# Moving ten weight splits from attention into the input stage of a hybrid attention and convolution trunk

## The chip, the cores and the metric

The kernel runs on one core of one Trainium2 chip. The metric is the device time of one execution in microseconds (us), as the median over several runs. The engines are named as in the profile: PE is TensorE's matrix unit (PEld its weight loads), DVE is VectorE, ACT is ScalarE, POOL is GpSimd, and SP is SyncE, which here issues nearly all transfers.

## The reference, cut to what matters

There are two layers over 1024 tokens of width 1024, each with a pre-norm and a residual add, and a final RMSNorm. The first layer is gated latent attention with 8 heads, the second a gated convolution module.

```python
z = h @ w_in                                   # layer 0: latents, rotary key, gate
q = (rmsnorm(q_lat, q_norm_g) @ w_qb)          # 8 heads of 128 + 64 rotary
kv = (rmsnorm(kv_lat, kv_norm_g) @ w_kvb)
o = causal_block_attention(q, k, v)
x = x + (o * silu(gate)) @ w_out
a, b, gate = split(h @ w_in + b_in, 3)         # layer 1: three projections
u = depthwise_conv31(a * sigmoid(b)) + dw_b
u = silu(layernorm(u, ln_g, ln_b))
x = x + (u * silu(gate)) @ w_out + b_out
return rmsnorm(x, final_norm_g)
```

What bears on the change are two weight matrices of layer 1: the gate columns of its input projection, in eight blocks called `cg0` to `cg7` (`wc[16]` to `wc[23]`), and its output projection, in eight blocks `e0` to `e7` (`we[0]` to `we[7]`). Each block is 128 by 1024 numbers of 4 bytes, 512 KB.

## The kernel before

**Two halves of every operand.** For precision each operand of a product is held as a high half in a rounded format (`hi`) and a low half, the difference (`lo = raw - hi`). A product is then three matmuls, `wh*xh`, `wh*xl` and `wl*xh`, at L138, L139 and L140 of `mm3`.

**Three ways to get a weight.** `load_w` loads a raw block, makes `hi` on ACT (L105) and `lo` on DVE or POOL (L107), and the halves are used at once. `split_early` (L113) is run long before the block is wanted: it loads the raw block, makes both halves in two pieces of 512 columns (L120 on ACT, L121 on the engine held in `early_eng`), and writes the low half alone to a DRAM tile `loS`. `load_split` is used in the last stages: it loads the raw block and the stored low half, and makes only the high half again (L134). So each of the sixteen blocks `cg0` to `cg7` and `e0` to `e7` is split once early, and its subtraction doesn't have to be done in the last stages.

**The buffers that all of them share.** A raw block takes a slot of tag `wraw`, of which there are 2. A high or low half takes a slot of tag `w`, of which there are 5. A slot is free again when its last reader is done: a raw slot after the subtraction, a high half of a split after the subtraction, a low half of a split after its transfer to DRAM, and the halves of a weight in use after the last matmul that reads them.

**The stages.** The input stage first accumulates the key and value latents over eight blocks of x (tile `acc`). Then come eleven calls of `in_tile`, each a gemm of 48 matmuls of 512 columns (tile `ps_b`) with weights from `w1b`: three for the query latents, then eight for the attention gate in `gate_tile(0)` to `gate_tile(7)`. Between gate tiles 5 and 6 stand two `rope_pair` calls (tile `ps_qr`), which need the normed query latents from `lat_norm` (tiles `Frq`, `rowq`, `Fq`, `zgq`, `qnh`, `qnl`). In this text the gate tiles are called g0 to g7. The attention stage follows: `proj(h)` (tile `pj`, weights `wqk[h]`, tile `wl_qk` for their low half), `score`, and `attend`, for eight heads. Then come the output projection of layer 0, the convolution layer, and the last stages that use `load_split`.

**What sets the order.** In the input stage, and after attention, PE's order is the order in which the code is written. Everywhere else a planner places the instructions on each engine before the program runs. It walks the program with a model of time and gives an engine, or SP's queue, what is ready and has a free slot; of two raw loads that want the same slot, the one written first goes first, as far as the trace before shows it. The order on each engine is then fixed, and an instruction that waits holds up all behind it on its engine.

**Where the splits stand.** Before the change `cg0` to `cg5` are split in the input stage, one behind each of g0 to g5, with `early_eng` on DVE. Behind g7 `early_eng` is set to POOL. `cg6` and `cg7` are split in heads 0 and 1, and `e0` to `e7` in heads 0 to 7, one in each, all on POOL.

Of the kernel before, what the change touches and what calls it, by code (L numbers as in the profile page):

```python
# [64 lines left out]
def hybrid_body(ctx, tc, xT, xP, pos, cols, w1a, w1b, wqr, wqk, wv, wo, wc, we, out):  # L65
    nc = tc.nc
    v, s, g, pe, sp = nc.vector, nc.scalar, nc.gpsimd, nc.tensor, nc.sync
# [28 lines left out]
    early_eng = [v]  # L96

    def load_w(src, n, nm, alloc=None, eng=None):
        if alloc is None:
            def alloc(name):  # L100
                return wp.tile([P, 1024], F32R, tag="w", bufs=5, name=name)
        raw = wp.tile([P, 1024], F32, tag="wraw", name=f"wr_{nm}")
        sp.dma_start(raw[:, :n], src)
        hi = alloc(f"wh_{nm}")
        s.activation(hi[:, :n], raw[:, :n], AF.Copy)  # L105
        lo = alloc(f"wl_{nm}")
        (eng or early_eng[0]).tensor_tensor(lo[:, :n], raw[:, :n], hi[:, :n].bitcast(F32), ALU.subtract)  # L107
        return hi, lo
# [4 lines left out]
    def split_early(src, nm):  # L113
        raw = wp.tile([P, 1024], F32, tag="wraw", name=f"sr_{nm}")
        sp.dma_start(raw, src)
        hi = wp.tile([P, 1024], F32R, tag="w", bufs=5, name=f"sh_{nm}")
        lo = wp.tile([P, 1024], F32R, tag="w", bufs=5, name=f"sl_{nm}")
        for a in range(2):
            cs = sl(a, CH)
            s.activation(hi[:, cs], raw[:, cs], AF.Copy)  # L120
            early_eng[0].tensor_tensor(lo[:, cs], raw[:, cs], hi[:, cs].bitcast(F32), ALU.subtract)  # L121
        loS[nm] = tc.dram_tile([P, 1024], F32, name=f"loS{nm}")
        sp.dma_start(loS[nm], lo.bitcast(F32))
# [13 lines left out]
    def mm3(ps, wh, wl, xh, xl, start, stop):  # L137
        pe.matmul(ps, wh, xh, start=start, stop=False)  # L138
        pe.matmul(ps, wh, xl, start=False, stop=False)  # L139
        pe.matmul(ps, wl, xh, start=False, stop=stop)  # L140
# [67 lines left out]
    def sl(k, n=P):  # L208
        return slice(k * n, (k + 1) * n)
# [23 lines left out]
    def tmp(nm):  # L233
        return ar.tile([P, T], F32, tag="tmp", bufs=4, name=nm)
# [4 lines left out]
    def pacc(nm):  # L239
        return pa.tile([P, CH], F32, tag="acc", bufs=6, name=nm)  # L240
# [72 lines left out]
    def lat_norm(zg, folded, n, gname, dh, dl, nm):  # L313
        F, part = folded
        ps = pstat(f"cs{nm}")[:, :32]
        pe.matmul(ps, mod32, part, start=True, stop=True)
        Fc = inv_sqrt(ps, 1.0 / (n * P), 1e-6, nm, extra=Rc)
        Fr = small.tile([P, 32], F32, tag="Fr", bufs=1, name=f"Fr{nm}")
        v.tensor_tensor(Fr, Fc, Rc, ALU.mult)
        spread_dma(Fr, T, F, nm)  # L320
        for i in range(n):
            v.scalar_tensor_tensor(zg[i], zg[i], cc(gname, i), F, ALU.mult, ALU.mult)
            s.activation(dh[i], zg[i], AF.Copy)
            v.tensor_tensor(dl[i], zg[i], dh[i].bitcast(F32), ALU.subtract)
# [11 lines left out]
    def in_tile(n):  # L336
        wh, wl = load_w(w1b[n], 1024, f"b{n}", eng=v)
        ps = []
        for c in range(2):
            ch = sl(c, CH)  # L340
            ps.append(pacc(f"ps_b{n}{c}"))
            for k in range(KD):
                mm3(ps[c], wh[:, sl(k)], wl[:, sl(k)], xgh[k][:, ch], xgl[k][:, ch],
                    k == 0, k == KD - 1)
        return ps
# [26 lines left out]
    def gate_tile(h):  # L372
        ps = in_tile(NQL + h)
        gt = tmp(f"gt{h}")
        for c in range(2):
            v.tensor_tensor(gt[:, sl(c, CH)], ps[c], R[:, sl(c, CH)], ALU.mult)
        s.activation(gt, gt, AF.Silu)
        sp.dma_start(gateS[h], gt)
# [6 lines left out]
    for h in range(3):  # L385
        gate_tile(h)
        split_early(wc[16 + h], f"cg{h}")
        if h == 2:
            lat_norm(zgq, folded, NQL, "gq", qnh, qnl, "q")

# [46 lines left out]
    def rope_pair(pr):  # L437
        ab = []
        for j in range(2):
            wh, wl = load_w(wqr[2 * pr + j], 384, f"qr{pr}{j}")  # L440
            t_ = ar.tile([P, T], F32, tag="zg", bufs=5, name=f"qr{pr}{j}")
            for c in range(2):
                ch = sl(c, CH)
                ps = pacc(f"ps_qr{pr}{j}{c}")
                for k in range(NQL):
                    mm3(ps, wh[:, sl(k)], wl[:, sl(k)], qnh[k][:, ch], qnl[k][:, ch],
                        k == 0, k == NQL - 1)
                s.activation(t_[:, ch], ps, AF.Copy, scale=QSCALE)
            ab.append(t_)
        A, B = ab  # L450
        for j in range(2):
            t1, t2 = tmp(f"rt1{pr}{j}"), tmp(f"rt2{pr}{j}")
            v.tensor_tensor(t1, A if j == 0 else B, cosT, ALU.mult)
            v.tensor_tensor(t2, B if j == 0 else A, sinT, ALU.mult)
            v.tensor_tensor(t1, t1, t2, ALU.subtract if j == 0 else ALU.add)
            hi = ar.tile([P, T], F32R, tag="rhi", bufs=1, name=f"rh{pr}{j}")
            s.activation(hi, t1, AF.Copy)
            v.tensor_tensor(t2, t1, hi.bitcast(F32), ALU.subtract)
            sp.dma_start(ropeS[j][pr], hi.bitcast(F32))
            sp.dma_start(ropeS[2 + j][pr], t2)  # L460

    for h in range(3, 6):
        gate_tile(h)
        split_early(wc[16 + h], f"cg{h}")
    rope_pair(0)
    rope_pair(1)
    gate_tile(6)
    gate_tile(7)

    early_eng[0] = g  # L470
    es_pe.close()
    es_ap.close()
    es_ax.close()
    es_ar.close()


    early = ctx.enter_context(tc.tile_pool(name="early", bufs=NFIRST, side="right",
                                           reuse_waits="tile"))
    es_b = ExitStack()
# [64 lines left out]
    def score(h, i):  # L544
        q_h, q_l, k_h, k_l, rq, _ = heads[h]
        nk = (i + 1) * P
        ps = psS_p.tile([P, T], F32, tag="S", name=f"S{h}_{i}")
        if i == 0:
            chunks, off = [(0, 256)], 0
        elif i == 4:  # L550
            chunks, off = [(0, 384), (384, 640)], 128
        else:
            chunks, off = [(a, min(a + CH, nk)) for a in range(0, nk, CH)], 0
        qs = sl(i)
        for a, b in chunks:
            o_ = ps[:, off + a : off + b]
            ks = slice(a, b)
            pe.matmul(o_, q_h[:, qs], k_h[:, ks], start=True, stop=False)
            pe.matmul(o_, q_h[:, qs], k_l[:, ks], start=False, stop=False)
            pe.matmul(o_, q_l[:, qs], k_h[:, ks], start=False, stop=False)  # L560
            pe.matmul(o_, rq[:, qs], krh[:, ks], start=False, stop=False)
            pe.matmul(o_, rq[:, qs], krl[:, ks], start=False, stop=True)
        st = b1.tile([P, 3], F32, tag="st", bufs=8, name=f"st{h}_{i}")
        last = ps[:, off + i * P : off + nk]
        v.tensor_tensor(last, last, mask, ALU.add)
        v.tensor_reduce(st[:, 0:1], ps[:, off : off + nk], AX.X, ALU.max, negate=True)  # L566
        pr = b1.tile([P, nk], F32, tag=f"P{i}", bufs=2 if i in (2, 3) else 1, name=f"P{h}_{i}")
        s.activation(pr[:, :nk], ps[:, off : off + nk], AF.Exp, bias=st[:, 0:1],  # L568
                     accum_out=st[:, 1:2])
        v.reciprocal(st[:, 2:3], st[:, 1:2])  # L570
        g.tensor_scalar(pr[:, :nk], pr[:, :nk], st[:, 2:3], 1.0, ALU.mult, ALU.mult)  # L571
        probs[h, i] = pr
# [46 lines left out]
    def load_og(grp, h, c):  # L619
        pair = act_tile(grp, f"og{c}{h}")  # L620
        sp.dma_start(pair[1].bitcast(F32), ogS[h][c])
        split_og(pair[1].bitcast(F32), pair)
        return pair
# [4 lines left out]
    for h in range(NH):  # L628
        for i in range(8):
            score(h, i)  # L630
            if i == 1 and pending is not None:
                attend(*pending)
                pending = None
            if i == 3 and h + 1 < NH:
                proj(h + 1)
            if i == 4 and h < 2:
                split_early(wc[22 + h], f"cg{6 + h}")
            if i == 6:
                split_early(we[h], f"e{h}")
            if i == 5:  # L640
                if h < NH - 1:
                    attend(h, 0)
                else:
                    ogt[0] = [load_og("A", h_, 0) for h_ in range(NH - 1)]
                    ogt[0].append(act_tile("A", f"og0{h}"))
                    attend(h, 0, ogt[0][h])
        pending = (h, 1)
# [499 lines left out]
```

## Time and profile before

| what | value |
|---|---|
| median of 3 runs | 906.93 us (906.04 to 909.69) |
| the profiled execution's own time | 906.78 us |
| its span, first to last instruction | 904.8 us |
| PE busy | 891.2 us, 98% of the span |
| DVE, ACT, POOL busy | 653.1, 503.5, 372.1 us |
| moved by DMA | 110.71 MB, mean 122 GB/s |

The span is what the trace covers, and 2 us of the execution's own time lie around it. PE's busy time overlaps itself, since matmuls are pipelined: a matmul of 512 columns is listed with some 0.40 us, but in a dense run the next one starts 0.23 us later. So the starts of matmuls tell more than the busy share. The input stage ends, and attention begins, with the first matmul of tile `pj`.

### The profile page before, as it was taken

Reading aid. Unit: us, or ns where it says so; the run is one execution under the profiler, and the core shown is the slowest. Engines: PE = TensorE matmul, PEld = TensorE weight load, DVE = VectorE, ACT = ScalarE, POOL = GpSimd, SP = SyncE. Lnnn points to the kernel's source line nnn. Section 1 sums busy time; section 2 is a strip of 40 time slices with the busy share of each in tenths; the row PEclk is TensorE's granted clock in tenths of the full one; section 3 lists DMA queues with packets and bytes.
Section 4 is the critical chain, followed back from the end, with each engine's and each line's share of the span. In section 5 each row is a group of like instructions: output and inputs, shape, how many; then the busy total and the mean of one; then the engine's idle time right before and its main releaser. Section 6 shows DMA issues by size and latency. Waiting matters only on the chain.

```text
span 904.8 us, 12389 instructions
## 1 busy us (share of the span) xinstructions
PE 891.2 (98%) x4416; PEld 743.1 (82%) x4416; DVE 653.1 (72%) x1114; ACT 503.5 (56%) x839; POOL 372.1 (41%) x335
## 2 busy tenths in 40 slices
PE   9999999999999999999999999999999999999996
PEld 7888887888988988988878778888888887778996
DVE  7788857556656666676454968999999997687543
ACT  8535355255645554574443457766666763678732
POOL 0000000143532522642334559999999992000034
PEclk9999999999999999999999999999999999999998
DMA  7325635572422430651363421111113323135714
GB/s 269 116 71 177 222 124 190 194 226 87 142 89 82 141 106 29 231 164 37 111 224 126 141 69 48 47 49 45 47 48 105 95 87 109 51 137 199 255 68 137
DMA packets 39837, 110.71 MB, mean 122 GB/s; under 512 B 5280, under 2 KB 8352, under 8 KB 39776
## 3 DMA queue, kind: packets, MB, share of 16 engines
q1 hardware_dynamic: 39408, 109.27, 36.2%
q8 instruction: 35, 0.57, 0.3%
q10 hardware_dynamic: 288, 0.39, 0.1%
q14 instruction: 26, 0.21, 0.1%
q0 software_dynamic: 80, 0.26, 0.1%
HBM read 83.93 MB, written 24.92 MB: 120 GB/s over the span
## 4 chain that ended last, share of the span: by engine, by line
PE 80%; DVE 3%; DMA 1%; ACT 1%; issue 1%; POOL 0%; DVEq 0%; SPq 0%; ACTq 0%; POOLq 0%
PE e L138 3%; PE e L140 3%; PE cb L139 3%; PE e L139 3%; PE cb L140 3%; PE T L584 3%; PE cb L138 3%; PE cg L138 3%; PE cg L139 3%; PE cg L140 3%; PE ca L138 3%; PE ca L140 3%; PE ca L139 3%; PE o L140 3%; PE o L138 3%; PE o L139 3%
## 5 line engine op out<-in xcount | busy, mean ns | idle before, releaser
L836 POOL TENSOR_TENSOR dcv<-dcv,pkb 128x512 f32<-128x512 f32 (+1 forms) x126 | 157.7, 1254 | 8.6 <-ACT pkb L835 1.0
L835 ACT ACTIVATE pkb<-u,taps 128x512 f32<-128x512 f32 (+1 forms) x126 | 83.6, 673 | 55.7 <-POOL dcv L836 50.9
L571 POOL TENSOR_SCALAR P<-P,st 128x128 f32<-128x128 f32 (+3 forms) x64 | 48.1, 753 | 120.7 <-DVE st L570 112.9
L847 DVE SCALAR_TENSOR_TENSOR av<-u,taps,av 128x512 f32<-128x512 f32 (+1 forms) x135 | 91.9, 689 | 1.2 <-ACT av L841 1.1
L107 POOL TENSOR_TENSOR wl_qk<-wr_qk,wh_qk 128x640 fp32r<-128x640 f32 x8 | 12.6, 1573 | 171.7 <-PE ps_b L139 165.1
L849 DVE SCALAR_TENSOR_TENSOR cv<-su,gsum,cv 128x512 f32<-128x512 f32 (+1 forms) x117 | 80.7, 690 | 0.4
L594 DVE TENSOR_TENSOR ptl<-T,pth 128x512 fp32r<-128x512 f32 (+1 forms) x96 | 52.3, 554 | 32.1 <-ACT pth L593 31.8
L593 ACT ACTIVATE pth<-T 128x512 fp32r<-128x512 f32 (+1 forms) x96 | 46.1, 490 | 52.3 <-PE T L584 45.3
L138 PE MATMUL ps_b<-xgh,wh_b 128*128 128x512 f32 x176 | 69.9, 397 | 0.0
L139 PE MATMUL ps_b<-xgl,wh_b 128*128 128x512 f32 x176 | 69.7, 396 | 0.0
L140 PE MATMUL ps_b<-xgh,wl_b 128*128 128x512 f32 x176 | 69.7, 396 | 0.0
L1026 POOL TENSOR_TENSOR x<-x,rbe 128x512 f32<-128x512 f32 (+1 forms) x16 | 16.2, 1043 | 126.8 <-DMA rbe<-rowe 121.6
L107 POOL TENSOR_TENSOR wl_o<-wr_o,wh_o 128x1024 fp32r<-128x1024 f32 x16 | 42.4, 2662 | 57.5 <-PE o L140 24.4
L138 PE MATMUL e<-a_y,wh_e 128*128 128x256 f32 (+1 forms) x192 | 61.8, 322 | 0.0
L140 PE MATMUL e<-a_y,wl_e 128*128 128x256 f32 (+1 forms) x192 | 61.6, 321 | 0.0
L139 PE MATMUL e<-a_y,wh_e 128*128 128x256 f32 (+1 forms) x192 | 61.4, 320 | 0.0
L568 ACT ACTIVATE P<-S,st 128x128 f32<-128x128 f32 (+3 forms) x64 | 47.5, 741 | 23.4 <-DVE st L566 18.7
L138 PE MATMUL cg<-a_h,wh_cg 128*128 128x512 f32 x128 | 51.7, 404 | 0.0
L139 PE MATMUL cb<-a_h,wh_cb 128*128 128x512 f32 x128 | 50.9, 397 | 0.8 <-DVE a_h L766 0.8
L140 PE MATMUL o<-a_og,wl_o 128*128 128x512 f32 x128 | 51.1, 399 | 0.3 <-POOL wl_o L107 0.3
L138 PE MATMUL o<-a_og,wh_o 128*128 128x512 f32 x128 | 51.0, 400 | 0.0
L138 PE MATMUL ca<-a_h,wh_ca 128*128 128x512 f32 x128 | 50.9, 397 | 0.0
(327 smaller groups left out, 2677.3 us busy)
## 6 DMA issues: line engine op xcount, KB each, us to landing
wr_o<-in_wo_dram SPq DMA_DIRECT2D x16, 512.0 KB, 3.9
wr_e<-in_we_dram SPq DMA_DIRECT2D x14, 512.0 KB, 4.6
wl_e<-loSe SPq DMA_DIRECT2D x14, 512.0 KB, 3.7
wr_b<-in_w1b_dram SPq DMA_DIRECT2D x11, 512.0 KB, 3.3
sr_cg<-in_wc_dram SPq DMA_DIRECT2D x8, 512.0 KB, 4.2
loScg<-sl_cg SPq DMA_DIRECT2D x8, 512.0 KB, 2.9
gateS<-gt SPq DMA_DIRECT2D x8, 512.0 KB, 4.3
rq<-ropeS SPq DMA_DIRECT2D x32, 128.0 KB, 2.8
```

The source lines that it names most:

```text
L107: (eng or early_eng[0]).tensor_tensor(lo[:, :n], raw[:, :n], hi[:, :n].bitcast(F32), ALU.subtract)
L138: pe.matmul(ps, wh, xh, start=start, stop=False)
L139: pe.matmul(ps, wh, xl, start=False, stop=False)
L140: pe.matmul(ps, wl, xh, start=False, stop=stop)
L568: s.activation(pr[:, :nk], ps[:, off : off + nk], AF.Exp, bias=st[:, 0:1], accum_out=st[:, 1:2])
L571: g.tensor_scalar(pr[:, :nk], pr[:, :nk], st[:, 2:3], 1.0, ALU.mult, ALU.mult)
L593: s.activation(hi[:, n0:], pt[:, n0:], AF.Copy)
L594: v.tensor_tensor(lo[:, n0:], pt[:, n0:], hi[:, n0:].bitcast(F32), ALU.subtract)
L835: s.activation(pk, lag(src, i), AF.Copy, scale=tap(of, i))
L836: g.tensor_tensor(acc, acc, pk, ALU.add)
L847: v.scalar_tensor_tensor(a_, lag(E, i), tap(dwe, i), a_, ALU.mult, ALU.add)
L849: v.scalar_tensor_tensor(c_, lag(su, i), tap(gsum, i), c_, ALU.mult, ALU.add)
```

## The change

Ten calls of `split_early` move from the head loop into the input stage. `e0` and `e1` are split behind g1 and g2, `e2` to `e4` behind g3 to g5, `cg6` and `cg7` behind g6 and g7, and `e5`, `e6`, `e7` behind that, with no gate tile between them. All sixteen are then worked out with `early_eng` on DVE. `early_eng` is set to POOL a few lines later than before, still ahead of attention. What each split loads, computes and stores is the same.

```diff
     for h in range(3):
         gate_tile(h)
         split_early(wc[16 + h], f"cg{h}")
+        if h > 0:
+            split_early(we[h - 1], f"e{h - 1}")
         if h == 2:
             lat_norm(zgq, folded, NQL, "gq", qnh, qnl, "q")
...
     for h in range(3, 6):
         gate_tile(h)
         split_early(wc[16 + h], f"cg{h}")
+        split_early(we[h - 1], f"e{h - 1}")
     rope_pair(0)
     rope_pair(1)
-    gate_tile(6)
-    gate_tile(7)
-
-    early_eng[0] = g
+    for h in range(6, 8):
+        gate_tile(h)
+        split_early(wc[16 + h], f"cg{h}")
+    for h in range(5, 8):
+        split_early(we[h], f"e{h}")
+
...
+    early_eng[0] = g
...
             if i == 3 and h + 1 < NH:
                 proj(h + 1)
-            if i == 4 and h < 2:
-                split_early(wc[22 + h], f"cg{6 + h}")
-            if i == 6:
-                split_early(we[h], f"e{h}")
```

## Rows read from the trace of the kernel before

**Rows 1.** The page's first part: busy us, share of the span, instructions.

```profile
PE 891.2 (98%) x4416; PEld 743.1 (82%) x4416; DVE 653.1 (72%) x1114; ACT 503.5 (56%) x839; POOL 372.1 (41%) x335
```

**Rows 2.** Windows: stretch, its us, busy us (instructions) by engine, clock, DMA.

```profile
core 0: us, PE busy (x) PEld busy (x) DVE busy (x) ACT busy (x) POOL busy (x), PEclk, DMA share, GB/s
60.00:180.00 120.00, 119.71 (x514) 96.27 (x514) 87.22 (x122) 52.63 (x69) 3.32 (x4) 1.00 0.51 175
180.00:380.00 200.00, 199.43 (x1183) 175.74 (x1181) 125.84 (x279) 110.63 (x244) 80.65 (x104) 1.00 0.38 120
...
160.00:180.00 20.00, 20.00 (x87) 16.11 (x87) 9.72 (x11) 5.46 (x7) 3.32 (x4) 1.00 0.51 185
```

**Rows 3.** Windows of 4 us at the kernel's start, the busiest for DMA.

```profile
12.00:16.00 4.00, 4.00 (x19) 3.22 (x18) 4.00 (x7) 4.00 (x6) 0.00 (x0) 1.00 1.05 405
```

**Rows 4.** Waits of PE, longest in total first: us, times, longest us.

```profile
PE bce L194 <- DVE rte L187: 1.3, 1, 1.3
```

**Rows 5.** Groups by line and shape: busy us, mean ns, idle before.

```profile
L121 POOL TENSOR_TENSOR sl_e<-sr_e,sh_e 128x512 fp32r<-128x512 f32 x16 | 20.4, 1296 | 2.1 <-ACT sh_e L120 1.1 <-PE pj L139 0.9
L121 DVE TENSOR_TENSOR sl_cg<-sr_cg,sh_cg 128x512 fp32r<-128x512 f32 x12 | 7.8, 687 | 2.0 <-PE ps_b L139 2.0
L120 ACT ACTIVATE sh_cg<-sr_cg 128x512 fp32r<-128x512 f32 x16 | 9.2, 624 | 15.7 <-DMA sr_cg<-in_wc_dram 15.7
L107 DVE TENSOR_TENSOR wl_b<-wr_b,wh_b 128x1024 fp32r<-128x1024 f32 x11 | 13.4, 1221 | 5.4 <-PE ps_b L139 3.0 <-ACT zgkv L328 2.4
L105 ACT ACTIVATE wh_b<-wr_b 128x1024 fp32r<-128x1024 f32 x11 | 11.6, 1056 | 10.3 <-PE acc L304 5.8 <-DMA wr_b<-in_w1b_dram 3.0 <-PE ps_b L140 1.5
L105 ACT ACTIVATE wh_qk<-wr_qk 128x640 fp32r<-128x640 f32 x8 | 5.9, 738 | 10.4 <-PE ps_b L140 8.7 <-DMA wr_qk<-in_wqk_dram 0.9 <-POOL sl_e L121 0.8
L107 POOL TENSOR_TENSOR wl_qk<-wr_qk,wh_qk 128x640 fp32r<-128x640 f32 x8 | 12.6, 1573 | 171.7 <-PE ps_b L139 165.1 <-PE pj L139 5.5 <-ACT wh_qk L105 0.6
```

**Rows 6.** DMA issues: count, KB each, median us from issue to landing.

```profile
sr_cg<-in_wc_dram SPq DMA_DIRECT2D x8, 512.0 KB, 4.2
...
wr_qk<-in_wqk_dram SPq DMA_DIRECT2D x8, 320.0 KB, 3.7
```

**Rows 7.** Tile `sr_e`, raw blocks split in attention: shortest, median, longest landing.

```profile
DMA to landing us min/median/max: 3.3/5.4/6.7
```

**Rows 8.** Timeline of PE: first matmuls of g2, of the rope, of g6, of attention.

```profile
92.72 0.40 PE L138 MATMUL ps_b<-xgh,wh_b 128*128 128x512 f32 x1
...
137.75 0.39 PE L138 MATMUL ps_qr<-qnh,wh_qr 128*128 128x512 f32 x1
...
155.16 0.40 PE L138 MATMUL ps_b<-xgh,wh_b 128*128 128x512 f32 x1
...
177.56 0.39 PE L138 MATMUL pj<-qnh,wh_qk 128*128 128x512 f32 x1
```

**Rows 9.** Timeline of DVE: the subtractions of `cg1`, then of g2's weights.

```profile
84.69 1.29 DVE L121 TENSOR_TENSOR sl_cg<-sr_cg,sh_cg 128x512 fp32r<-128x512 f32 x2
...
88.82 1.22 DVE L107 TENSOR_TENSOR wl_b<-wr_b,wh_b 128x1024 fp32r<-128x1024 f32 x1
```

**Rows 10.** Timeline of SP: loads of g2's weights, a rope weight, head 0's weights.

```profile
76.88 0.33 SPq L103 DMA_DIRECT2D wr_b<-in_w1b_dram  x1
...
134.58 0.38 SPq L103 DMA_DIRECT2D wr_qr<-in_wqr_dram  x1
...
154.08 0.38 SPq L103 DMA_DIRECT2D wr_qk<-in_wqk_dram  x1
```

**Rows 11.** Chain that ended last, by time: start us, us, what.

```profile
121.38 4.23 DMA rowq<-Frq
125.62 3.61 DMA Fq<-rowq
129.32 1.13 issue
130.46 2.48 DVE zgq L322 x2
132.94 1.20 DVE sl_cg L121 x2
...
138.06 0.57 DVE wl_qr L107
```

## The prediction, made before the changed kernel ran

> **What bounds the kernel.** I read the page's totals first, then the windows of the two stages that the change touches, then the waits of PE, then the timelines around each gate tile. PE is busy 98% of the span [rows 1], and with pipelined matmuls that alone proves nothing. The windows are better: from 60 to 180 us, where six splits run today, PE has 0.29 us without work in 120, and from 180 to 380 us, where the ten others run, 0.57 us in 200 [rows 2]. Its longest wait of the whole span is 1.3 us, near the end [rows 4]. So PE sets the time in both stages, and nothing that another engine does is on the path unless it makes PE wait. The question is therefore not what a split costs, but whether ten more of them make PE's next weights late in the input stage, and whether PE waits for any of them today.
>
> **What is removed.** Twenty POOL subtractions leave attention, 16 of them on `e` blocks at 1296 ns [rows 5]; with the four on `cg` blocks at the same size that is 20 x 1.30 = 26 us of POOL, and 20 x 0.62 = 12 us of ACT. POOL is busy 80.65 of 200 us there and ACT 110.63 [rows 2], so neither is near full, and PE's idle time in that stretch is 0.57 us in all. The gain lies between nothing and 0.57 us; I take 0.4, because the small waits of PE are on the probabilities, which come from ACT and DVE, and ACT is relieved. Ten raw loads and ten stores of 512 KB leave too; PE waits for no transfer there.
>
> **What is added to engines.** Each split costs DVE two subtractions of 687 ns, as `cg` today, 1.3 us with their overlap [rows 5, 9], and ACT 2 x 0.62 = 1.2 us. Ten of them are 13 us of DVE and 12 us of ACT in 120 us of input stage, where DVE is busy 87 and ACT 53 [rows 2]. On average there is room. The subtraction itself is half as long as on POOL. This costs nothing as a sum; it costs where an order or a slot makes it so. Three places have little room.
>
> **First place, the gate tiles g2 to g5.** A tile lasts 11.2 us, (177.56 - 155.16) / 2 [rows 8]. In it the two raw slots served two blocks (a split and the next gate's weights); with `e0` to `e4` they serve three. A split holds its raw slot for some 4.2 us of landing, 0.3 of issue, 1.2 of ACT and 1.3 of DVE, 7.0 us [rows 5, 6, 9, 10]. Three are 21 us of 22.4 us of slot time: it fits, with hardly anything to spare. With the longest landing seen for such a block, 6.7 us [rows 7], three are 28.5 us and each tile would come (28.5 - 22.4) / 2 = 3 us late. So four tiles cost between 0 and 12 us. For g2 it can be followed: its raw block went out at 76.88 us [rows 10] into a slot that `e0`, written earlier, now takes; the next slot comes free when `cg1` is subtracted, at 84.69 + 1.29 = 85.98 us. Issue, 4.2 of landing, 1.06 of ACT and 1.22 of DVE give 92.8 us, where the low half was ready at 90.04 before [rows 5, 6, 9]. PE begins g2 at 92.72 and wants the low half two matmuls later, at 93.2 [rows 8]. That is just in time. I take 0.25 us a tile, 1.0 in all, near the lower bound, since landings of 4.2 us are the rule in this stage.
>
> **Second place, the start of the rope.** Here the chain of waits left PE and ran over `rowq`, `Fq`, `zgq` and `wl_qr` [rows 11]; PE began at 137.75 [rows 8], while the low rope weight was subtracted from 138.06 to 138.63, so this place is already late by 0.4 us. The first rope weight stands in SP's queue and in the raw slots behind `cg5`, and now behind `e4` too. If it gets the slot that `cg5` leaves at 134.1 us, as the second rope weight did (134.58 [rows 10]), it lands some 3.7 us later, as the block of 320 KB does [rows 6], and with 1.1 us of halving it is ready at 139.4, 0.8 us later than before. The norm chain in front has two more splits, 2.4 us of DVE and 2.4 of ACT, to share engines with; half a microsecond of that I take to reach PE. At most the chain slips by one whole transfer that stands in front of its square root on ACT, 5.5 us or so. So 0 to 6 us, and I take 1.2.
>
> **Third place, head 0's projection.** PE begins it at 177.56 us [rows 8], and its raw weights went out at 154.08 [rows 10], long before. Now five blocks are written ahead of it and want the raw slots first: `cg6`, `cg7`, `e5`, `e6`, `e7`. Of the five `w` slots g6 and g7 hold four until g6 ends at 155.16 + 11.2 = 166.4 us. The fifth holds the high half of `cg7`, whose low half has no slot, and so `e5` to `e7` cannot be finished. From 166.4 on: `cg7` subtracted at 167.7 and its raw slot given to `e6`; `e6` lands 5.4 us later (the median of these blocks in attention [rows 7], since transfers now crowd), 173.1; 1.2 of ACT and the last 0.7 of DVE, 175.0; the slot goes to head 0's weights, 3.7 to land [rows 6], 178.7; ACT makes the high half in 0.74 [rows 5], 179.4; POOL the low half in 1.57, 181.0. PE wants the low half two matmuls into the projection, at 178.0. It waits 3.0 us. With the longest landing for both blocks, 6.7 us each, it is 4.3 more. If head 0's weights stay ahead of `e6`, it is nothing. So 0 to 7.3 us, and I take 3.7, a bit above the middle value, for the crowding.
>
> That crowding can be weighed. From 160 to 180 us DMA moves 185 GB/s, 3.7 MB [rows 2]; four splits add 4 x 2 x 0.524 = 4.2 MB, so 7.9 MB in 20 us, 395 GB/s. The most that a stretch of this trace moved is 405 GB/s [rows 3], so it just fits. The Trainium skill's page "DMA: Bandwidth & Descriptors", section Specifications, puts what HBM gives one core at some 358 GB/s. The row above moved more than that from 12 to 16 us, so the measurement decides here. By the page the same bytes would take 22.1 us, 2.1 us over the stretch, and my sum would be 2.1 us higher.
>
> **Sum.** The profiled execution took 906.78 us, 0.15 under the median of 906.93. 906.78 - 0.4 + 1.0 + 1.2 + 3.7 = 912.3 us, 0.6% slower.
>
> **Rivals.**
>
> *Nothing is late (not slower).* The place is head 0's weights. If the planner's model of time gives them a raw slot before `e6`, or if `e6` leaves its slot by 178.0 - 1.57 - 0.74 - 3.7 = 172.0 us, the 3.7 us go, and the other two terms are within what their lower bounds allow. For it: loads are placed early wherever a slot allows, as the 23 us lead before shows. Against it: five blocks are written in front. 906.8 - 0.4 + 1 to 2, some 908 us.
>
> *DVE's queue (slower).* From 122 to 129 us DVE had nothing placed in front of `zgq` and stood waiting for `Fq` [rows 11]; `cg5`, which could have run, was behind it. g5's low half was subtracted just before that wait. With `e3` in front it can fall behind `zgq`, at about 133 + 1.2 = 134 us, for a tile that wants it at 127: 7 us. The rest of the sum shrinks, since the rope then begins later anyway: 906.8 - 0.4 + 1 + 7 + 3.7 = 918.
>
> *Transfers at their ceiling.* If 395 GB/s cannot be held beside SP's other work, both landings in the third place are 6.7 us [rows 7] and PE waits 7.3 there: 916 us. The page named above speaks for it.
>
> *The clock.* TensorE's granted clock is at its upper level, 1.00, in every window [rows 2, 3], and no wait of PE is over 1.3 us [rows 4], so no row shows what follows a wait of 3 us or more. If the clock falls to 1.2 GHz behind it, a half tile of 5.6 us takes 11.2: 918 us. The Trainium skill's page "TensorE: Matmul & The Clock Gate", Part 1, says that the engine's clock is halved after idle time and comes back with sustained work; nothing in this trace bears it out or denies it.
>
> *Faster.* Without the splits attention's order is planned anew, and its three matmul patterns could fit closer. PE's idle time there, 0.57 us, bounds this near 906; more needs a denser order, of which I see no sign.
>
> **How the numbers follow.** Chances: forecast 0.40 (own range 909 to 916), nothing late 0.28, DVE's queue 0.12, transfers 0.08, clock 0.07, faster 0.05. Half a per cent, about what a measurement of this kernel can tell from no change, is 4.5 us, so the bounds are 902.4 and 911.5 us. The forecast lies just above the upper one; I give it 0.24 slower and 0.16 same. Slower: 0.24 + 0.12 + 0.08 + 0.07 = 0.51. Same: 0.16 + 0.28 = 0.44. Faster: 0.05. The range leaves out the faster case, the better end of nothing late and the worst of the DVE and clock cases: 906.3 to 920.5 us.
>
> **What would show it.** Right: a wait of PE of 2 to 5 us before the first `pj` matmul, with `wr_qk` issued after about 174 us; g2's low half within a microsecond of its use; PE's idle time in attention as small as before, with POOL 26 us less busy. Wrong: `wr_qk` issued well before g6 ends; `wl_b` of g5 behind `zgq` on DVE; a granted clock under 1.00; or matmuls in attention in a tighter order, so that head 7 ends earlier relative to the first `pj`.

## The result, and the profile after

| | before | after |
|---|---|---|
| median of 4 runs | 906.66 us (906.04 to 909.69) | 928.05 us (926.20 to 928.88) |
| the profiled execution, its span | 906.78, 904.8 us | 927.44, 925.6 us |

The ratio of the times is 1.022, with a 95% interval of 1.0202 to 1.0238: 2.2% slower. The forecast was 912.3 us in a range of 906.3 to 920.5, so the sign was right, but the time lies outside the range, and the loss is four times the size.

The page's totals of the changed kernel answer to [rows 1]. PE, with as many matmuls as before, is listed with 6.9 us more of work, and DVE and POOL show the subtractions that changed sides. The second line is the granted clock in forty slices: one slice at 7, under full speed, lies at 185 to 208 us.

```profile
PE 898.1 (97%) x4416; PEld 745.6 (81%) x4416; DVE 666.3 (72%) x1134; ACT 505.2 (55%) x839; POOL 346.2 (37%) x315
...
PEclk9999999979999999999999999999999999999998
```

The waits of PE name the places. Before, the first row was the 1.3 us of `bce` [rows 4]; now three others stand ahead of it, all in the input stage and at its end.

```profile
PE pj L138 <- ACT wh_qk L105: 7.0, 1, 7.0
PE ps_b L140 <- DVE wl_b L107: 3.4, 3, 2.4
PE ps_b L138 <- ACT wh_b L105: 2.6, 2, 1.5
PE bce L194 <- DVE rte L187: 1.3, 1, 1.3
```

These make 13.0 us, and the span grew by 20.8. What is missing is found by following the start of each tile on PE through both traces:

| first matmul of | before | after | late by |
|---|---|---|---|
| g2 | 92.72 | 92.81 | 0.1 |
| g3 | 104.06 | 106.09 | 2.0 |
| g4 | 115.35 | 119.73 | 4.4 |
| g5 | 126.55 | 132.55 | 6.0 |
| rope | 137.75 | 147.82 | 10.1 |
| g6 | 155.16 | 164.69 | 9.5 |
| head 0's projection (`pj`) | 177.56 | 194.28 | 16.7 |
| the first scores (`S`) | 184.86 | 204.24 | 19.4 |
| the layer's output projection (`o`) | 421.78 | 441.55 | 19.8 |
| end of span | 904.8 | 925.6 | 20.8 |

Nearly all of it comes in two steps: 10.0 us between g2 and the rope, and 9.9 between g6 and the first scores. In the first step PE's timeline shows these waits, behind a short one of 0.40 us in g2 (at 93.84), the largest of them at g5. The wait at `pj` belongs to the second step.

```profile
106.09 0.50 PE L138 MATMUL ps_b<-xgh,wh_b 128*128 128x512 f32 x1 [1.11 <-ACT wh_b L105]
...
107.35 0.50 PE L140 MATMUL ps_b<-xgh,wl_b 128*128 128x512 f32 x1 [0.53 <-DVE wl_b L107]
...
132.55 0.50 PE L138 MATMUL ps_b<-xgh,wh_b 128*128 128x512 f32 x1 [1.45 <-ACT wh_b L105]
...
135.71 0.80 PE L140 MATMUL ps_b<-xgh,wl_b 128*128 128x512 f32 x1 [2.43 <-DVE wl_b L107]
...
194.28 0.79 PE L138 MATMUL pj<-qnh,wh_qk 128*128 128x512 f32 x1 [7.03 <-ACT wh_qk L105]
```

The rest is the clock. The windows below (columns as in [rows 2]; `PEclk` is the last but two) are three stretches in which the granted clock is at its lower level, 0.50, that is 1.2 GHz, and then the 20 us around the third.

```profile
107.80:111.20 3.40, 3.40 (x10) 2.61 (x9) 3.40 (x7) 2.11 (x4) 0.00 (x0) 0.50 0.74 231
135.10:138.50 3.40, 2.79 (x7) 2.21 (x8) 2.89 (x4) 0.42 (x1) 0.00 (x0) 0.50 0.89 299
189.70:200.00 10.30, 5.72 (x14) 4.38 (x15) 1.21 (x2) 2.37 (x4) 3.26 (x4) 0.50 1.04 331
...
180.00:200.00 20.00, 12.97 (x46) 9.87 (x45) 7.37 (x11) 7.32 (x10) 3.26 (x4) 0.74 1.01 330
```

Each begins where PE has just waited: behind 1.11 and 0.53 us at g3, within the 2.43 us at g5, behind the 1.45 there, and within the 7.0 us at `pj`. At half the clock, half of the time in which PE works is lost. That is 1.7 us in the first stretch and 1.4 in the second, where PE starts again at 135.71. Behind `pj` the projection takes 9.96 us up to the first scores, 7.30 before: 2.7 more. The first step is then 6.0 us of waits (the two `ps_b` rows) and 3.1 of clock, with about 1 in small gaps around the waits; the second is 7.0 of waits and 2.7 of clock. Before, the clock was 1.00 in every stretch shown [rows 2]. The Trainium skill's page "TensorE: Matmul & The Clock Gate", Part 1, says that the clock is halved after idle time and returns with sustained work. These three stretches agree with it; the last section has waits behind which the clock didn't fall.

Attention itself gained nothing. From the first scores to the first `o` it takes 237.31 us, and took 236.92 before, though POOL is busy there 25.4 us less. The two windows, before and after:

```profile
184.86:421.78 236.92, 235.41 (x1388) 206.62 (x1387) 154.34 (x339) 134.97 (x295) 95.66 (x123) 1.00 0.38 121
...
204.24:441.55 237.31, 235.35 (x1389) 206.47 (x1387) 154.54 (x339) 126.05 (x276) 70.25 (x103) 1.00 0.22 71
```

Why the weights of `pj` are late is read backwards through three engines. SP's timeline has the load of `e6`, that of `e7`, and head 0's weights, which went out at 154.08 before [rows 10]:

```profile
178.13 0.71 SPq L115 DMA_DIRECT2D sr_e<-in_we_dram  x1
181.99 0.94 SPq L115 DMA_DIRECT2D sr_e<-in_we_dram  x1
187.04 0.85 SPq L103 DMA_DIRECT2D wr_qk<-in_wqk_dram  x1
```

DVE's timeline has the subtractions of `cg7` and of `e6`, whose ends make the raw slots free:

```profile
176.40 1.28 DVE L121 TENSOR_TENSOR sl_cg<-sr_cg,sh_cg 128x512 fp32r<-128x512 f32 x2
...
184.68 1.28 DVE L121 TENSOR_TENSOR sl_e<-sr_e,sh_e 128x512 fp32r<-128x512 f32 x2
```

ACT's timeline has the high half of `e6`, and that of head 0's weights, 0.79 us before PE begins:

```profile
183.48 1.15 ACT L120 ACTIVATE sh_e<-sr_e 128x512 fp32r<-128x512 f32 x2
...
193.49 0.74 ACT L105 ACTIVATE wh_qk<-wr_qk 128x640 fp32r<-128x640 f32 x1 [3.38 <-DMA wr_qk<-in_wqk_dram]
```

So: g6 ends at 175.9; `cg7` is subtracted by 177.68; its raw slot goes to `e6`, subtracted by 185.96; the slot that this leaves goes to head 0's weights, which take 6.4 us from issue to landing.

### The profile page after: what moved, and what is told of

Read it like the earlier page. It is cut to its first block, busy times and chain, and to the rows that moved or that the text cites. A ratio compares the mean times of both kernels' runs of the same rounds, so it can differ in the third digit from the quotient of the medians.

```text
span 925.6 us, 12373 instructions
## 1 busy us (share of the span) xinstructions
PE 898.1 (97%) x4416; PEld 745.6 (81%) x4416; DVE 666.3 (72%) x1134; ACT 505.2 (55%) x839; POOL 346.2 (37%) x315
## 4 chain that ended last, share of the span: by engine, by line
PE 74%; DVE 5%; DMA 4%; ACT 2%; issue 1%; POOL 1%; SPq 0%; DVEq 0%; ACTq 0%; POOLq 0%
PE e L138 3%; PE e L140 3%; PE T L590 3%; PE cb L139 3%; PE e L139 3%; PE cb L140 3%; PE cb L138 3%; PE cg L138 3%; PE cg L139 3%; PE cg L140 3%; PE ca L138 3%; PE ca L140 3%; PE ca L139 3%; PE o L140 2%; PE pj L138 2%; PE o L138 2%
## 5 line engine op out<-in xcount | busy, mean ns | idle before, releaser
L139 PE MATMUL cb<-a_h,wh_cb 128*128 128x512 f32 x128 | 50.8, 397 | 0.8 <-DVE a_h L768 0.8
L138 PE MATMUL cb<-a_h,wh_cb 128*128 128x512 f32 x128 | 50.8, 397 | 0.0
```

## The experiments

Each time is a median with the ratio to the kernel before, which ran beside it on the same chip (its medians there were 906.85 to 907.47 us), and its 95% interval. Starts and waits are from one profiled execution of each kernel. Diffs are cut, and are against the kernel that is named.

**One half of the change at a time.** In the first kernel (tail_only) `e0` to `e4` go back into the heads, so that the tail alone (`cg6`, `cg7`, `e5` to `e7` behind g6 and g7) is moved. Against the kernel after:

```diff
     for h in range(3):
-        if h > 0:
-            split_early(we[h - 1], f"e{h - 1}")
...
     for h in range(3, 6):
-        split_early(we[h - 1], f"e{h - 1}")
...
+            if i == 6 and h < 5:
+                split_early(we[h], f"e{h}")
```

> Only cg6, cg7, e5, e6 and e7 are split in the input stage; e0 to e4 stay in heads 0 to 4 on POOL as before. If the loss sits in two separate places (some 10 us in the gate tiles, some 10 us ahead of head 0's projection: a wait of 7 us and a slow clock behind it), g2 to g5 start at the times of before, PE waits some 7 us for head 0's high half, and the time is 916 to 918 us. If the wait ahead of head 0 is only the sequel of late gate tiles, whose transfers bunch up behind them, it falls under 2 us here and the time is 906 to 910 us.

Measured 918.07 us, 1.0121 [1.0098, 1.0143]. The rope begins on time at 137.81, and the wait at `pj` is there in full, as PE's waits say. The second row, for the probabilities in attention, has grown from 1.0 us in the kernel after; its cause stays open.

```profile
PE pj L138 <- ACT wh_qk L105: 7.0, 1, 7.0
PE S L561 <- ACT P L571: 3.1, 2, 2.2
```

The second kernel (gates_only) moves the other half alone. Against the kernel before:

```diff
     for h in range(3):
+        if h > 0:
+            split_early(we[h - 1], f"e{h - 1}")
...
     for h in range(3, 6):
+        split_early(we[h - 1], f"e{h - 1}")
...
-            if i == 6:
+            if i == 6 and h >= 5:
```

> Only e0 to e4 move into the input stage, behind g1 to g5; cg6, cg7 and e5 to e7 stay in the heads on POOL. With two separate places: the starts of g3, g4 and g5 are late as in the changed kernel, by 2 to 6 us, the rope by some 10 us, the projection of head 0 finds its weights ready, and the time is 916 to 918 us. If late gate tiles alone made everything late, the wait ahead of head 0 would come here too, and the time would be 923 to 928 us.

Measured 916.69 us, 1.0102 [1.0082, 1.0121]. PE starts g3 at 105.50, g5 at 132.0 and the rope at 148.25, and `pj` without a wait. The waits are those of the changed kernel but for `pj`:

```profile
PE ps_b L140 <- DVE wl_b L107: 3.4, 3, 2.4
PE ps_b L138 <- ACT wh_b L105: 3.1, 2, 2.3
```

The two halves lose 1.2% and 1.0%, together what the change loses: two separate places.

**Head 0's weights ahead of `e5` to `e7`.** In this kernel (head0_first) the three splits are written behind `proj(0)`. Against the kernel after:

```diff
-    for h in range(5, 8):
-        split_early(we[h], f"e{h}")
...
     proj(0)
+    early_eng[0] = v
+    for h in range(5, 8):
+        split_early(we[h], f"e{h}")
+    early_eng[0] = g
```

> As the changed kernel, but e5, e6 and e7 are written behind the call that loads head 0's weights, still on DVE. If the order in which blocks get the two raw slots makes head 0 wait, the wait of 7 us goes, with the slow clock behind it, and the time is 917 to 920 us. If the transfers at their ceiling make it wait, the same bytes still move in the same stretch, the wait stays over 4 us and the time over 923 us.

Measured 921.47 us, 1.0162 [1.0137, 1.0187]. The weights go out 17 us earlier, and `pj` begins at 186.88 with no wait:

```profile
169.66 0.38 SPq L103 DMA_DIRECT2D wr_qk<-in_wqk_dram  x1
```

Nearly the same bytes are moved in that stretch (318 GB/s from 165 to 205 us, 339 in the kernel after), so it was the order of the slots that made `pj` wait, and not a ceiling of the transfers alone. The first scores come 10.1 us earlier than in the kernel after, the end of the span 7.9, and the median lies above the 917 to 920 us that were expected: a part of the gain is lost again. PE waits 3.1 us in all for the probabilities of head 0. The longest of these waits, 1.7 us, ends with `P` below. In front of it ACT takes the high half of a late `e` block, for whose load it stands still, and DVE the low half, before the `st` that `P` needs:

```profile
204.01 1.15 ACT L120 ACTIVATE sh_e<-sr_e 128x512 fp32r<-128x512 f32 x2 [2.28 <-DMA sr_e<-in_we_dram]
...
205.87 0.58 ACT L571 ACTIVATE P<-S,st 128x384 f32<-128x384 f32 x1 [0.71 <-DVE st L569]
```

**PE kept busy while it waits.** To price the clock alone, in pe_kept_busy 9, 18 and 31 extra matmuls of 512 columns, whose result nobody reads, are put in front of g3, g5 and `pj` in the kernel after:

```diff
+    def keep_pe(n, nm):
+        ps = pstat(f"keep{nm}")
+        for _ in range(n):
+            pe.matmul(ps, xgh[0][:, :P], xgh[0][:, :CH], start=True, stop=True)
...
+        if h in (3, 5):
+            keep_pe({3: 9, 5: 18}[h], f"g{h}")
...
+    keep_pe(31, "p")
```

> The changed kernel with 9, 18 and 31 matmuls of 512 columns whose results nobody reads, ahead of g3, of g5 and of head 0's projection, about as long as PE waits there (2.1, 4.2 and 7.2 us). If the waits bring the granted clock down and the slow clock costs some 6 us beside the waits, the clock is 1.00 throughout and the time is 920 to 924 us. If the slow clock costs nothing of its own, the time stays at 926 to 930 us.

Measured 924.12 us, 1.0189 [1.0164, 1.0214]. The interval overlaps that of the kernel after, 1.0202 to 1.0238, so the total alone can't price the clock; the span of the profiled execution, 921.0 us, is 4.6 shorter. The windows around the two places are at full clock now:

```profile
100.00:140.00 40.00, 38.36 (x165) 30.47 (x164) 29.46 (x43) 20.80 (x27) 0.00 (x0) 1.00 0.69 245
180.00:205.00 25.00, 24.56 (x120) 19.86 (x119) 10.97 (x19) 9.93 (x15) 3.28 (x4) 1.00 0.95 317
```

So PE's idleness brings the clock down in these places, and work that means nothing keeps it up. Of the 5.8 us assigned to the clock above 3.0 come back by the first scores: the rope begins 1.0 us earlier and the first scores 3.0. Where the other 1.6 us of the span come from stays open. At the gates most of the slow time had cover: g4 ends about 1.1 us earlier here, but the low half that g5 waits for is used at 136.02, no earlier than the 135.71 of the kernel after.

**What holds up the gates: DVE, raw slots or `w` slots?** First DVE is relieved (pool_early): in the kernel after, `e0` to `e4` are subtracted on POOL (one of the two loops is shown).

```diff
+            early_eng[0] = g
             split_early(we[h - 1], f"e{h - 1}")
+            early_eng[0] = v
```

> The changed kernel with the subtractions of e0 to e4 on POOL, which has no other work in the input stage. If DVE's crowded queue makes the weights of g3 to g5 late, the rope starts at least 5 us earlier than in the changed kernel and the time is 918 to 923 us. If it is the time that a block holds its raw slot, POOL's longer subtraction (1.3 us against 0.7 for each half) makes it no better, 926 to 932 us.

Measured 930.93 us, 1.0254 [1.0225, 1.0282], and the rope at 149.26: no better. This doesn't clear DVE. The two subtractions of a block take 2.6 to 3.5 us on POOL here, for 1.3 on DVE, so slots are held longer. And two operations of DVE that ran beside POOL's first subtraction took 1.47 and 1.77 us, where the same ones took 0.70 in the kernel after. That DVE's work alone isn't the cause is shown by all_apart below: there DVE does all these subtractions, and nothing is late.

Then (own_slot) the `e` blocks get a raw slot of their own, half a block long, so that they no longer compete for the two. In the kernel after, all eight `e` blocks:

```diff
+    def split_own(src, nm):
+        hi = wp.tile([P, 1024], F32R, tag="w", bufs=5, name=f"sh_{nm}")
+        lo = wp.tile([P, 1024], F32R, tag="w", bufs=5, name=f"sl_{nm}")
+        for a in range(2):
+            cs = sl(a, CH)
+            raw = ar.tile([P, CH], F32, tag="sraw", name=f"sr_{nm}{a}")
+            sp.dma_start(raw, src[:, cs])
...
-        split_early(we[h - 1], f"e{h - 1}")
+        split_own(we[h - 1], f"e{h - 1}")
```

> The changed kernel, but e0 to e7 load their raw block in two halves of 512 columns into one slot of their own, so that the two raw slots serve gates, cg blocks and head 0 alone, as before. All else, the five slots for halves, DVE and the bytes moved, is as in the changed kernel. If the raw slots make PE's weights late, g2 to g5 start within a microsecond of before, head 0's wait is under 2 us and the time is 907 to 912 us. If the five slots, DVE's queue or the transfers do it, most of the waits stay and the time is 918 to 928 us.

Measured 934.19 us, 1.0285 [1.0268, 1.0302]: worse. The rope begins at 146.63, 1.2 us earlier than in the kernel after and still 8.9 late, and PE then waits 13.3 us for head 0's high half. The gates' high halves now wait on ACT for a `w` slot, which comes free when the low half of a `cg` block has been stored:

```profile
103.11 1.06 ACT L105 ACTIVATE wh_b<-wr_b 128x1024 fp32r<-128x1024 f32 x1 [3.17 <-DMA loScg<-sl_cg]
```

A split in two loads, one behind the other, can also hold its `w` slots longer, so this run says that raw slots alone aren't the whole cause, and no more.

The next two start from gates_only. One (halves_apart) keeps `split_early`'s whole raw block, but takes the halves of the `e` blocks from the `tmp` slots of another pool; the other (all_apart) takes the raw halves from a slot of their own as well. The edit of the first, against it, and then what the second adds:

```diff
+    def split_apart(src, nm):
+        hi = ar.tile([P, T], F32R, tag="tmp", bufs=4, name=f"sh_{nm}")
+        lo = ar.tile([P, T], F32R, tag="tmp", bufs=4, name=f"sl_{nm}")
+        raw = wp.tile([P, 1024], F32, tag="wraw", name=f"sr_{nm}")
...
-            split_early(we[h - 1], f"e{h - 1}")
+            split_apart(we[h - 1], f"e{h - 1}")
```

```diff
-        raw = wp.tile([P, 1024], F32, tag="wraw", name=f"sr_{nm}")
-        sp.dma_start(raw, src)
...
+            raw = ar.tile([P, CH], F32, tag="sraw", name=f"sr_{nm}{a}")
+            sp.dma_start(raw, src[:, cs])
```

> As gates_only (e0 to e4 in the input stage, the others in the heads), but the high and low halves of e0 to e4 take slots of tag tmp instead of the five w slots; their raw blocks still take the two raw slots. In gates_only the rope starts 10 us late. If the w slots make the gate weights late, it starts under 3 us late and the time is 907 to 910 us. If the raw slots do, it stays 8 to 11 us late and the time is 914 to 918 us. If it takes both, it lies between.

> As halves_apart, and the raw blocks of e0 to e4 come in halves of 512 columns through a slot of their own, so that these blocks take neither raw nor w slots. What they still share with the gate weights are DVE's, ACT's and SP's queues and the transfers. If slots of either kind are the whole cause, g2 to g5 and the rope start on time and the time is 906 to 909 us. If the queues or the transfers are it, the rope is still over 4 us late and the time over 911 us.

The first: 917.56 us, 1.0108 [1.0077, 1.0139], the rope at 151.19, 13.4 us late: nothing gained. The second: 907.31 us, 0.9998 [0.9985, 1.0011], no loss left. Its windows, for [rows 2], show the five blocks in the input stage (DVE 93.39 where it was 87.22, 217 GB/s where it was 175) and PE without work for only 0.17 us of 120; its timeline has the rope and `pj` at their old times:

```profile
60.00:180.00 120.00, 119.83 (x515) 96.18 (x514) 93.39 (x132) 58.46 (x79) 3.37 (x4) 1.00 0.63 217
180.00:380.00 200.00, 199.57 (x1184) 175.91 (x1184) 126.75 (x280) 105.23 (x234) 68.49 (x94) 1.00 0.30 94
```

```profile
137.59 0.39 PE L150 MATMUL ps_qr<-qnh,wh_qr 128*128 128x512 f32 x1
...
177.27 0.39 PE L150 MATMUL pj<-qnh,wh_qk 128*128 128x512 f32 x1
```

With the same work on the same engines, and the buffers apart, the loss of the gates is gone. Both kinds of slots bind: with the `w` slots free (halves_apart) the rope is as late as ever, so raw slots alone are enough for the loss, and with the raw blocks of `e` in a slot of their own (own_slot) it is still 8.9 us late. And POOL's work in attention fell, while the time stayed: the splits cost nothing there.

**The gates' weights written ahead of the `e` block.** If the order in which slots are given is the cause, it should help to ask for the next gate's weights first (gates_ahead). Against gates_only:

```diff
+    def load_in(n):
+        ahead[n] = load_w(w1b[n], 1024, f"b{n}", eng=v)
...
         split_early(wc[16 + h], f"cg{h}")
+        if h < 5:
+            load_in(NQL + h + 1)
         split_early(we[h - 1], f"e{h - 1}")
```

> As gates_only (e0 to e4 in the input stage, the rest in the heads), but the weights of the next gate tile are written ahead of the e block, so that they are given a raw slot first. If the order in which the blocks get the slots is the cause, g3 to g5 start on time, and the 916.7 us of gates_only come down to 907 to 910 us; the e blocks are then the late ones. If there is too little room whatever the order (slots for halves, transfers), it stays at 913 to 917 us.

Measured 912.20 us, 1.0056 [1.0038, 1.0074], between the two cases: half of the gates' loss goes. g3 and g4 begin 0.4 us ahead of their old times (103.63, 114.92). g5 waits 0.5 us for its high half and 2.1 for its low half, and the rope begins at 141.42, 3.7 us late. The low half stands behind `zgq` and `qnl` in DVE's order:

```profile
120.87 3.67 DVE L322 SCALAR_TENSOR_TENSOR zgq<-zgq,col,Fq 128x1024 f32<-128x1024 f32 x3
...
125.06 3.48 DVE L324 TENSOR_TENSOR qnl<-zgq,qnh 128x1024 fp32r<-128x1024 f32 x3
...
128.46 1.22 DVE L107 TENSOR_TENSOR wl_b<-wr_b,wh_b 128x1024 fp32r<-128x1024 f32 x1
```

The same order with the halves of the `e` blocks in `tmp` slots too (apart_ahead, which is halves_apart with the same edit):

> As halves_apart, with the weights of the next gate tile written ahead of the e block, as in gates_ahead (912.2 us). There g3 and g4 came on time and g5 waited 2.1 us for its low half. If what was left there came from the w slots, g5 and the rope start within a microsecond of before and the time is 906 to 908 us, at best 0.6 us under before, since PE's idle time in attention is no more. If g5's low half is late because of its place in DVE's queue, the wait stays and the time is 910 to 913 us.

Measured 910.21 us, 1.0040 [1.0022, 1.0059]. g3 to g5 are on time (g5 at 126.33), and the rope is 1.7 us late at 139.43, since its weights have to wait for a raw slot. The time fell into the range of the second case, but the wait of g5 went, as in the first. So what held up g5 in gates_ahead began at the `w` slots: with them free, g5's raw load goes out at 117.71, not at 119.98, and DVE's order has its low half, at 122.70, ahead of `zgq`.

**The two `cg` blocks alone (cg_only).** Against the kernel before, only `cg6` and `cg7` move, behind g6 and g7:

```diff
-    gate_tile(6)
-    gate_tile(7)
+    for h in range(6, 8):
+        gate_tile(h)
+        split_early(wc[16 + h], f"cg{h}")
...
-            if i == 4 and h < 2:
-                split_early(wc[22 + h], f"cg{6 + h}")
```

> Only cg6 and cg7 move, one behind each of g6 and g7; e0 to e7 stay in the heads. If it takes three and more blocks behind the last gate tile to make head 0's weights late, PE doesn't wait there and the time is that of before within 2 us. If each block in front costs its share of the 7 us, PE waits 2 to 3 us there and the time is 909 to 912 us.

Measured 906.94 us, 0.9991 [0.9980, 1.0003], `pj` at 177.35 with no wait. Of the five blocks ahead of head 0's weights, two alone cost nothing.

**All ten, with the `e` blocks apart (all_sixteen_apart).** Against all_apart, `e0` to `e7` stand behind g0 to g7 in buffers of their own, `cg6` and `cg7` behind g6 and g7:

```diff
-        if h > 0:
-            split_apart(we[h - 1], f"e{h - 1}")
+        split_apart(we[h], f"e{h}")
...
-        split_apart(we[h - 1], f"e{h - 1}")
+        split_apart(we[h], f"e{h}")
...
-    gate_tile(6)
-    gate_tile(7)
+    for h in range(6, 8):
+        gate_tile(h)
+        split_early(wc[16 + h], f"cg{h}")
+        split_apart(we[h], f"e{h}")
...
-            if i == 4 and h < 2:
-                split_early(wc[22 + h], f"cg{6 + h}")
-            if i == 6 and h >= 5:
-                split_early(we[h], f"e{h}")
```

> All ten splits leave attention, as in the changed kernel, but e0 to e7 stand one behind each of g0 to g7 and take neither raw nor w slots (a half raw slot of their own, halves in tag tmp); cg6 and cg7 stand behind g6 and g7 as in the changed kernel. Two narrower kernels, all_apart (e0 to e4 so) and cg_only, took the time of before. If the splits cost nothing once they take no slot from the gate tiles' and head 0's weights, PE doesn't wait ahead of head 0 and the time is 905 to 909 us; that attention is then free of POOL's subtractions gains at most 0.6 us. If all ten together are too much for the queues or for the tmp slots of the rope, PE waits at the rope or ahead of head 0 and the time is 911 us or more.

Measured 926.01 us, 1.0211 [1.0195, 1.0226], a miss. The gates and the rope are on time (rope 137.51, g7 166.25), and head 0's weights go out at 161.87 in time. But PE waits 3.4 us for DVE's eviction of a gate tile (`gt`) before it begins `pj` at 181.01, and 13.7 us within `pj`:

```profile
PE pj L150 <- DVE ql L535: 13.7, 1, 13.7
PE pj L150 <- DVE gt L388: 3.4, 1, 3.4
```

`ql` and `qh` evict the first `pj` tiles, which PE had finished by 187.0. ACT's timeline has `qh` behind the high halves of late `e` blocks, for whose loads ACT stands still:

```profile
194.66 0.63 ACT L132 ACTIVATE sh_e<-sr_e 128x512 fp32r<-128x512 f32 x1 [4.75 <-DMA sr_e<-in_we_dram]
198.66 0.63 ACT L132 ACTIVATE sh_e<-sr_e 128x512 fp32r<-128x512 f32 x1 [3.37 <-DMA sr_e<-in_we_dram]
199.20 1.06 ACT L534 ACTIVATE qh<-pj 128x512 fp32r<-128x512 f32 x2
```

The loss has moved, from the slots into the order of ACT and DVE. That no other kernel with all ten splits in buffers of their own would do better isn't shown. The Trainium skill's page "Perfetto Trace Analysis", section "Tensor Engine Instruction", calls these engines' queues strictly first in, first out; the rows agree: `qh` runs only when the split in front of it has its data.

## Why the prediction had the places right and the sizes wrong

**What bounds the kernel: right.** PE sets the time, and what the splits cost as work counts nowhere: five of them fit the input stage without a trace (all_apart), two more at its end (cg_only). What counts is what makes PE wait. That the sign came out as well owes something to luck: the forecast gave "slower" 0.51, and the term that should have carried it, the third place's 3.7 us, was a little over a third of what the place cost.

**Attention, forecast -0.4 us: no gain.** It took 0.4 us more, in one execution of each. With half the splits gone (all_apart) the whole time is 0.9998 of before.

**First place, forecast +1.0: 10.0 us. The step that failed is the 7.0 us for which a split was to hold its raw slot, and with it the choice of 0.25 us a tile "near the lower bound, since landings of 4.2 us are the rule".** The 7.0 us add up a load, ACT's work and DVE's, and count nothing for standing behind other work. g2 went nearly as worked out: its low half was to be ready at 92.8, was ready at 93.78, and PE waited 0.4 us. But I followed only g2, the first of four. In the kernel after, `e0` was loaded at 77.15, its high half was made by 82.96, and its subtraction stood behind other work of DVE until 90.51. It held its slot 13.4 us, and g3's raw load went out at 99.72, 9.7 us later than before (90.07).

```profile
77.15 0.33 SPq L115 DMA_DIRECT2D sr_e<-in_we_dram  x1
...
89.21 1.30 DVE L121 TENSOR_TENSOR sl_e<-sr_e,sh_e 128x512 fp32r<-128x512 f32 x2
...
99.72 0.33 SPq L103 DMA_DIRECT2D wr_b<-in_w1b_dram  x1
```

From issue to the end of the subtraction, the splits from `e0` to `cg5` held their slots 8.8 us on average, and the blocks of g2 to g5 8.4. Landings are a part of that: those of g3 to g5 took 5.2, 5.2 and 6.9 us. With 8.66 us, the mean of these twelve blocks, for 7.0 the prediction's own formula gives (26.0 - 22.4) / 2 = 1.8 us a tile. That is an estimate, and it fits: without the 3.1 us of clock the four tiles lost 6.9. The sum also left out the `w` slots, three blocks of two halves each, against five, of which the running tile holds two; own_slot and all_apart show that they bind too. The bounds, 0 to 12 us, did hold the whole.

**Second place, forecast +1.2: nothing of its own.** From the rope's start to g6 PE took 0.5 us less than before. The norm chain had 10 us more time, because the gates in front were late. The terms were added as if a delay in front didn't give time to what comes behind.

**Third place, forecast +3.7: 9.9 us. The links were right, and the term too small.** From the end of g6 to the high half I worked out 13.0 us (166.4 to 179.4), and 18.3 passed (175.9 to 194.2). Of the 5.3 us more, 3.8 lie in the last load (7.5 us from the free slot to data, for 3.7, of which 1.1 passed before SP issued it and 6.4 until it had landed), 0.6 in DVE coming later to `e6`, 0.4 in `e6`'s load with its issue, 0.5 in `cg7`. The high half was to be 1.8 us late, so 7.1; PE waited 7.0. My upper end, 7.3, lay closest to it, though it was made up otherwise, of two landings of 6.7 us. The 2.7 us of clock come on top, and the sum had nothing for them.

**The rivals.** *Nothing is late*: refuted at both places. *DVE's queue*: real, as a part. In the kernel after, g5's high half is made by 132.49, but its low half is subtracted at 134.44 only, behind `zgq` at 127.97 and two pieces of `qnl`, and PE waits 2.43 us for it, where 7 were forecast. It is the sequel of a late load (issued at 124.10, landed at 131.0): apart_ahead and all_apart have no wait at g5. *Transfers at their ceiling*: in part. head0_first moves nearly the same bytes with no wait at `pj`, so the order makes that wait. But landings did grow under the load: head 0's weights took 6.4 us, for 3.7 [rows 6], and that is 2.7 of the 9.9 us, while `e6` took 5.3, about the 5.4 that were worked out. *The clock*: it fell, not as an alternative but behind both losses. That was the error in the table of cases: a fall of the clock and a late weight were given as rivals, with chances that exclude each other, where the one follows from the other. The trace of the kernel before could have told, at its end, where the prediction read only the wait: PE waits 0.69 and 1.27 us there, at 895.24 and 897.12, and from 898 us on its clock is 0.50.

**Open.** Whether any order hides all ten splits: none of the orders tried beat the kernel before, and with attention unmoved by five splits less there is little to win. Own_slot mixes two effects. The planner also placed each kernel's work anew, so that orders on ACT, DVE and SP differ from run to run (`zgq` begins at 127.97 in the kernel after, at 130.74 in all_apart). That freeing the `w` slots and the raw slots together, and not some third effect of the two shorter loads, is what cures the gates is the plainest reading of three runs, but a kernel with whole raw blocks in a slot of their own beside separate halves wasn't run.

## What to carry to other kernels

Work that is done ahead of its need competes with the critical loads for buffers and for places in engine queues, not only for engine time: before moving it, follow every pool slot through all the tiles it passes, not the first one, and look at what stands behind it in order on ACT and DVE. Read how long a slot is held off the trace, from the load's issue to the end of its last reader; a sum of the parts leaves out the standing in queues. A wait of PE can cost more than its length, since the granted clock may fall behind it; price both together. And where the bottleneck engine shows half a microsecond of idle time in 200, relieving another engine there is worth nothing.

## What was not expected of the hardware

The clock fell behind short waits, but not behind all of them. PE waited 1.45 us ahead of g5 and 2.43 us two matmuls later, and from within the second wait on the clock was 0.50 for 3.4 us; at g3 waits of 1.11 and 0.53 us, two matmuls apart, went before the same. In other kernels waits like these left it at 1.00: 0.78 and 0.53 us at g3 in gates_only, 0.50 and 2.05 at g5 in gates_ahead, and a single 2.22 us in tail_only. So the length of a wait alone doesn't tell here whether the clock will fall. Matmuls without meaning kept it at 1.00. And one core moved 330 GB/s for 20 us at the end of the input stage (the window from 180 to 200 us above), while a block took over 6 us to arrive, as the transfers issued from 160 to 200 us show (count, KB each, median us from issue to landing; compare [rows 6]):

```profile
sr_e<-in_we_dram SPq DMA_DIRECT2D x3, 512.0 KB, 6.1
...
wr_qk<-in_wqk_dram SPq DMA_DIRECT2D x3, 320.0 KB, 6.5
```
